# A second mixer whose recurrence is projected before its heads, and first feed-forward products taken by token tile

## The chip, the cores and the metric

The kernel runs on one core of a Trainium2 chip. TensorE (PE in the profile, its weight loads PEld), VectorE (DVE), ScalarE (ACT), GpSimd (POOL) and SyncE (SP) each work through a list of instructions of their own and wait for each other by semaphores. The metric is the time on the device of one execution, in microseconds (us). Three runs of the kernel before took 1424.63, 1426.79 and 1426.91 us; the median is 1426.79 us.

## The reference

Two transformer blocks follow each other on 256 tokens of width 1024, all in float32. The first (latent attention and stick-breaking heads, 32 experts of which each token takes four, a gated embedding) is not touched by the change but for its last norm. The second is, cut to what matters (dimension checks, transposes and casts left out):

```
def second_block(x, ...):
    h = rms_norm(x, g_pre_mix)
    q, k, v, xr, gr = split(h @ w_in)                    # five times 512 columns
    attn = moba_attention(q, k, v, rel_bias)             # 8 heads of 64; at 256 tokens plain causal
                                                         # softmax attention with a bias by distance
    xr = causal_dwconv(xr, w_conv_lru, b_conv_lru)       # 4 taps
    lru = rg_lru(xr, ...) * gelu(gr)
    mix = concatenate([attn, lru]) @ w_out               # 1024 x 1024
    x = x + rms_norm(mix, g_post_mix)
    h = rms_norm(x, g_pre_ffn)
    up = causal_dwconv(h @ w_up, w_conv_ffn, b_conv_ffn) # 5632 columns, 3 taps
    c_u, c_g = split(up)
    ffn = (gelu(c_g) * c_u) @ w_down
    return x + rms_norm(ffn, g_post_ffn)

def rg_lru(x, w_r, b_r, w_i, b_i, lam):                  # along the tokens
    r = sigmoid(x @ w_r + b_r); i = sigmoid(x @ w_i + b_i)   # block-diagonal, 8 blocks of 64
    log_a = -8 * r * softplus(-lam)
    u = sqrt(-expm1(2 * log_a)) * (i * x)
    h[t] = exp(log_a[t]) * h[t - 1] + u[t]
```

## The kernel before, in words

The tokens are two tiles of 128. Where a product has its output by feature, both token tiles stand side by side as 256 columns. A float32 operand is split into a high part in fp32r (ACT copies it, `wh` or `uh`) and the rest (`wl` or `ul`, one subtraction on DVE, L257 for weights); a product is then three matmuls, high by high, and twice high by low (`mm3`, L272 to L275). `mm_T` (L268) does so over the eight chunks of 128 inputs: 24 matmuls for 128 features. Weights come in pieces of 2 MB through a ring of three buffers, in the order of `plan` (`want`, L197 to L205); SP issues the next load when `done` frees a buffer.

The program is written in one order per step, and a scheduler that lays out the lists of all engines together moves instructions past each other where their operands allow it; `issue_after` holds some back. What stands where is seen from the lists below.

The second block runs thus. `x2_norm` (L1300) ends the first block's last norm and leaves the scale `rB` that the projections' outputs are multiplied by. `v` is projected first, then sixteen steps of `mm_T` (loop at L1465, `seq`) project `q`, `k`, `xr` and `gr`, four steps each. Two steps make a pair of 128-feature chunks, and behind a pair comes what it is for: a scaled copy to `qT` or `kT`; for `xr` the convolution (`conv`, L1347); for `gr` the gate products and the first half of the recurrence (`lru_gates`, `lru_a`). The heads are a generator (`attention`, L1439): scores `a_s`, transposes of the probabilities `a_t`, and for each pair of heads the output `a_o` into `mxh` and `mxl`; it is advanced twice behind each step of `xr` and `gr`. `lru_b` (L1374) ends the recurrence: square root, gelu, scan, gate.

`nat2` (L1202) then multiplies by `w_out`: the half with the heads (48 matmuls of 512 columns, written first), then the recurrence's half, token tile 0 before token tile 1 (24 each), and behind each tile its norm (`epi2`, L1540). While tile 1 is multiplied, DVE and ACT take tile 0 through the norms (`norm_head`, `norm_tail`, `scale3`); `turn3` (L1531) transposes it by PE and splits it to `uh`, `ul`. Between the transposes of tile 0 and those of tile 1 stand 24 matmuls into a tile that nobody reads (L1548 to L1550). The feed-forward loop follows: 44 steps `mm_T` of 256 columns, convolution, gelu, and the products with `w_down`. Its first four steps are written before the loop into `pre`. Of the first up weights, piece 0 is split by POOL, and piece 1's rest too (L1507).

Of the kernel before, what the change touches and what calls it, by code (L numbers as in the profile page):

```python
# [36 lines left out]
P = 128  # L37
# [67 lines left out]
def block_kernel(ctx: ExitStack, tc: tile.TileContext, A, out, dbg=None, parts=("t1", "moe", "over", "t3")):  # L105
# [93 lines left out]
    wo2 = A["w_o2"].rearrange("(c k p) n -> c p k n", p=P, k=4)  # L199
    for c in range(2):  # L200
        want(("o2", c), wo2[c], [P, 4, 1024])
# [994 lines left out]
    def acc_tile():  # L1196
        return psq.tile([P, 512], FT, name="acc")
# [162 lines left out]
    def lru_a(hf):  # L1360

        ms = slice(2 * hf, 2 * hf + 2)
        if hf == 0:
            held["a"] = mx_.tile([P, 4, S], FT, name="xr")
        a_ = held["a"]
        for m in (2 * hf, 2 * hf + 1):
            act(a_[:, m], rg[:, m], AF.Exp, scale=ch[:, m:m + 1], bias=ch[:, m:m + 1])
            ts(rg[:, m], rg[:, m], ch[:, m:m + 1], ch[:, m:m + 1], OP.mult, OP.add)
        stt(ig[:, ms], ig[:, ms], 1.0, xc[:, ms], OP.add, OP.mult)
        act(rg[:, ms], rg[:, ms], AF.Tanh, scale=-1.0)  # L1370
        act(xc[:, ms], a_[:, ms], AF.Square)
        stt(xc[:, ms], xc[:, ms], 1.0, rg[:, ms], OP.add, OP.mult)
# [48 lines left out]
    def a_o(p):  # L1421
        o = acc_tile()
        for kb in range(2):
# [34 lines left out]
    def presplit(j):  # L1458
        if j < len(seq):
            i, hf, m = seq[j][0]  # L1460
            sp[j] = split(ws, seq[j][1]())
            if hf == 1 and m == 1:
                done(("in2", i))

    heads = attention()  # L1465
    presplit(0)
    presplit(1)
    for j, ((i, hf, m), _) in enumerate(seq):
# [6 lines left out]
        if m == 1:  # L1475
            if i == 1:
                stt(qT[:, sl], ps, 0.125, rB2, OP.mult, OP.mult)
            elif i == 2:
                tt(kT[:, sl], ps, rB2, OP.mult)
            elif i == 3:  # L1480
                tt(xr[:, sl, 3:3 + S], ps, rB2, OP.mult)
                conv(2 * hf)
                conv(2 * hf + 1)
            else:
                tt(gr[:, sl], ps, rB2, OP.mult)
                lru_gates(2 * hf)
                lru_gates(2 * hf + 1)
                lru_a(hf)
        if i >= 3:
            next(heads, None)  # L1490
            next(heads, None)
    for _ in heads:
        pass
    lru_b()
    for m in range(4):
        act(mxh[:, 4 + m], gr[:, m])
        tt(mxl[:, 4 + m], gr[:, m], mxh[:, 4 + m].bitcast(FT), OP.subtract)
    uh, ul = new_u(t3)
# [3 lines left out]

    first = [row_split(("o2", 0), i) for i in range(4)]
    done(("o2", 0))
    wdn, wup, acts = {}, {}, {}

    def split_up(i):  # L1507
        if i >= 44:
            return
        j, m = divmod(i, 2)  # L1510
        if i in (1, 2):
            hi, lo = [mx_.tile([P, 8, P], FR, name=n) for n in (("xc", "ig"), ("rg", "vN"))[i - 1]]
            src = src_T(("up", 0), j % 2, m)
            act(hi, src)
            (G if i < 2 else V).tensor_tensor(out=lo, in0=src, in1=hi.bitcast(FT), op=OP.subtract)
            wup[i] = hi, lo
        else:
            wup[i] = split(ws, src_T(("up", j // 2), j % 2, m), eng=G if i < 1 else V)
        if i % 4 == 3:
# [20 lines left out]
    def epi2(t, acc):  # L1540
# [14 lines left out]
    for i in range(3):  # L1555
# [74 lines left out]
def host_arrays(inputs):  # L1630
# [110 lines left out]
```

## Time and profile before

| | |
|---|---|
| median of 3 runs | 1426.79 us |
| the profiled execution | 1425.2 us |
| its span | 1423.4 us |
| PE busy in the span | 1315.6 us (92%) |
| DVE busy | 627.9 us (44%) |
| ACT busy | 370.3 us (26%) |
| POOL busy | 38.9 us (3%) |
| DMA moved | 482.39 MB |

Shares of the whole span mix two parts. Up to about 1080 us the experts' weights stream in and PE waits for them; behind that the weights come faster than they are used. The change lies in the last 320 us, so the rows below are from there: windows, waits and single instructions. A matmul's duration in a row reaches to the end of its results; where matmuls follow each other, the distance from start to start is what each takes of PE.

### The profile page before, as it was taken

What the parts mean: (1) busy time and instruction counts of PE and PEld (TensorE: products, weight loads), DVE (VectorE), ACT (ScalarE), POOL (GpSimd) and SP (SyncE); (2) the same over time, 40 slices, a digit from 0 to 9 for tenths busy, and PEclk for the clock granted to TensorE, in tenths of its full rate; (3) what the DMA queues carried; (4) which work ended last, traced back from release to release, by engine and by line L of the source; (5) the groups of instructions that cost most, each with busy time, mean ns of one, the idle gap of its engine ahead of it and who ended that gap; (6) DMA issues with size and microseconds to landing.
All of it is one profiled execution on the core that took longest, in us unless ns stands there. A gap on an engine that the chain in (4) does not pass through costs nothing.

```text
span 1423.4 us, 19768 instructions
## 1 busy us (share of the span) xinstructions
PE 1315.6 (92%) x8361; PEld 741.2 (52%) x8362; DVE 627.9 (44%) x1250; ACT 370.3 (26%) x639; POOL 38.9 (3%) x53
## 2 busy tenths in 40 slices
PE   6999999999998899889999888998888998999997
PEld 6877543433433333333343333333335886899997
DVE  5576533332322223223232222322225878677776
ACT  5545310101100101001010001000014658555554
POOL 1010200000000000000000000000000101000000
PEclk9999999999999999999999999999999999999999
DMA  7339899999999999999999999999998533355530
GB/s 283 112 106 375 324 420 427 427 427 426 425 428 427 428 426 425 427 413 426 427 428 427 427 427 427 427 426 426 428 426 350 192 126 134 135 195 198 198 148 30
DMA packets 40654, 482.39 MB, mean 339 GB/s; under 512 B 4104, under 2 KB 4640, under 8 KB 12656
## 3 DMA queue, kind: packets, MB, share of 16 engines
q1 hardware_dynamic: 38944, 477.58, 80.8%
q0 software_dynamic: 752, 2.36, 0.5%
q8 instruction: 67, 1.10, 0.3%
q10 hardware_dynamic: 864, 1.13, 0.2%
q14 instruction: 27, 0.22, 0.0%
HBM read 479.99 MB, written 1.06 MB: 338 GB/s over the span
## 4 chain that ended last, share of the span: by engine, by line
DMA 47%; PE 46%; DVE 4%; ACT 1%; issue 1%; POOL 1%; DVEq 0%; SPq 0%; ACTq 0%; POOLq 0%
DMA w<-w_gu 27%; DMA w<-w_dn 19%; PE gu L978 9%; PE y L1014 5%; PE acc L273 3%; PE acc L274 3%; PE acc L275 3%; PE wk L274 3%; PE wk L275 3%; PE wk L273 3%; PE pj L273 2%; PE pj L275 2%; PE pj L274 2%; PE xg L948 1%; PE tr L993 1%
## 5 line engine op out<-in xcount | busy, mean ns | idle before, releaser
L978 PE MATMUL gu<-w,xg 128*64 128x512 f32 x2048 | 471.6, 603 | 44.7 <-DMA w<-w_gu 38.1
L978 PEld LDWEIGHTS gu<-w,xg 128*64 128x64 f32 x2048 | 142.0, 137 | 315.9 <-issue 248.9
L1014 PE MATMUL y<-w,gl 128*64 128x512 f32 x1024 | 233.1, 597 | 28.4 <-DMA w<-w_dn 26.7
L121 ACT ACTIVATE h<-gu,gs 128x512 f32<-128x512 f32 x64 | 40.5, 683 | 559.5 <-PE gu L978 559.5
L124 DVE TENSOR_TENSOR h<-sc,h 128x512 f32<-128x512 f32 x126 | 81.3, 686 | 203.2 <-PE sc L1038 200.7
L257 DVE TENSOR_TENSOR wl<-w,wh 128x1024 fp32r<-128x1024 f32 (+2 forms) x124 | 148.2, 1205 | 46.4 <-ACT wh L121 45.9
L1014 PEld LDWEIGHTS y<-w,gl 128*64 128x64 f32 x1024 | 72.9, 136 | 161.1 <-issue 156.4
L121 ACT ACTIVATE wh<-w 128x1024 fp32r<-128x1024 f32 (+2 forms) x125 | 128.3, 1038 | 96.9 <-PE acc L275 21.6
L124 DVE TENSOR_TENSOR gl<-tr,bgu 128x512 f32<-128x512 f32 x32 | 22.1, 691 | 269.5 <-PE tr L993 269.5
L274 PE MATMUL wk<-ul,wh 128*128 128x256 f32 x336 | 94.5, 281 | 0.2 <-DVE ul L124 0.2
L273 PE MATMUL wk<-uh,wh 128*128 128x256 f32 x336 | 94.5, 281 | 0.0
L275 PE MATMUL wk<-uh,wl 128*128 128x256 f32 x336 | 94.3, 281 | 0.0
L121 ACT ACTIVATE sg<-gl 128x512 f32<-128x512 f32 x32 | 20.1, 630 | 182.8 <-DVE gl L131 176.1
L274 PEld LDWEIGHTS wk<-ul,wh 128*128 128x128 f32 x336 | 63.4, 189 | 1.2 <-DVE ul L124 0.4
L273 PEld LDWEIGHTS wk<-uh,wh 128*128 128x128 f32 x336 | 63.3, 188 | 1.0 <-ACT uh L121 0.2
L275 PEld LDWEIGHTS wk<-uh,wl 128*128 128x128 f32 x336 | 63.4, 189 | 0.0
L963 DVE CAST gt<-y 128x256 fp32r<-128x256 f32 x32 | 13.6, 424 | 112.8 <-PE y L961 112.8
L948 PE MATMUL xg<-oh,u 128*128 128x64 bf16 x1536 | 50.0, 193 | 0.7 <-ACT proj L121 0.7
L948 PEld LDWEIGHTS <-u 128*128 128x128 bf16 x1536 | 49.1, 98 | 2.6 <-issue 2.3
L127 DVE SCALAR_TENSOR_TENSOR cv<-wk,vec,cv 128x255 f32<-128x255 f32 x88 | 42.2, 480 | 8.7 <-ACT cv L121 7.1
L127 DVE SCALAR_TENSOR_TENSOR sg<-y,gs,li 128x512 fp32r<-128x512 f32 x31 | 23.3, 750 | 49.9 <-ACT li L121 49.9
L121 ACT ACTIVATE li<-y,gs 128x512 fp32r<-128x512 f32 x31 | 21.3, 687 | 80.7 <-PE y L1014 79.2
(410 smaller groups left out, 1748.3 us busy)
## 6 DMA issues: line engine op xcount, KB each, us to landing
w<-w_gu SPq DMA_DIRECT2D x128, 2048.0 KB, 39.1
w<-w_dn SPq DMA_DIRECT2D x63, 2048.0 KB, 39.1
w<-w_up SPq DMA_DIRECT2D x11, 2048.0 KB, 8.1
w<-w_in SPq DMA_DIRECT2D x7, 2048.0 KB, 10.5
w<-w_down SPq DMA_DIRECT2D x5, 2048.0 KB, 7.5
w<-w_o SPq DMA_DIRECT2D x4, 2048.0 KB, 8.6
w<-w_pg SPq DMA_DIRECT2D x2, 2048.0 KB, 35.3
w<-w_in SPq DMA_DIRECT2D x2, 1024.0 KB, 9.2
```

The costliest lines, as they stand in the source:

```text
L121: return SC.activation(out=o, in_=i, func=f, **kw)
L124: return V.tensor_tensor(out=o, in0=a, in1=b, op=op)
L127: return V.scalar_tensor_tensor(out=o, in0=a, scalar=s, in1=b, op0=op0, op1=op1)
L257: eng.tensor_tensor(out=lo, in0=src, in1=hi.bitcast(FT), op=OP.subtract)
L273: PE.matmul(o, l[0], r[0], start=first, stop=False)
L274: PE.matmul(o, l[0], r[1], start=False, stop=False)
L275: PE.matmul(o, l[1], r[0], start=False, stop=last)
L948: PE.matmul(px[:, kd], u3[i][:, t, kd * P:(kd + 1) * P], oh[:, t], start=(n == 0), stop=(n == 5))
L963: V.tensor_copy(gt, pgt[:, 0:S])
L978: PE.matmul(ps[64 * s:64 * s + 64, n], xg[:, k], w[:, kk, s * 1024 + n * 512:s * 1024 + (n + 1) * 512], start=(k == 0), stop=(k == 7))
L993: PE.transpose(pt[:, m], hf[:, m * P:(m + 1) * P], ident)
L1014: i = PE.matmul(ps[64 * s:64 * s + 64], aT[:, k], w[:, kk, s * 512:(s + 1) * 512], start=(k == 0), stop=(k == 7))
```

## The change

The order of projections becomes `v`, `xr`, `gr`, then the first halves of `q` and `k`, then the second halves; the packing of `w_in2` on the host follows it. `lru_b` and its split stand behind the last step of the first halves. The heads are advanced twice behind each of the last four projection steps, and once behind each half-chunk of `w_out`'s recurrence half, which now comes first and is accumulated in four PSUM tiles held from there on. The heads' half comes second, tile 0 before tile 1 as before. The 24 matmuls of L1550 are gone; in their place `pre_up(0)` does the four first feed-forward steps for token tile 0 (128 columns), and `pre_up(1)` does them for tile 1 behind `turn3(1)`. POOL splits nothing any more: the four first up pieces are split by ACT and DVE, in buffers of the mixer. `a_o` takes its PSUM tile from the `wk` buffers, not the `acc` ones. Two small edits: `x2_norm` folds two scalings into one pass, and the recurrence's `Tanh` takes its scale and bias from columns instead of a DVE pass.

```
-    for c in range(2):
+    for c in (1, 0):
         want(("o2", c), wo2[c], [P, 4, 1024])
...
+    ts(nch, ch, -1.0, None, OP.mult)
...
     def x2_norm(t):
-        tt(xn[:, t], xn[:, t], gfin, OP.mult)
+        stt(xn[:, t], xn[:, t], r1[:, t:t + 1], gfin, OP.mult, OP.mult)
-        ts(ss, ss, r1[:, t:t + 1], r1[:, t:t + 1], OP.mult, OP.mult)
-        ts(xn[:, t], xn[:, t], r1[:, t:t + 1], None, OP.mult)
...
-            ts(rg[:, m], rg[:, m], ch[:, m:m + 1], ch[:, m:m + 1], OP.mult, OP.add)
+            act(rg[:, m], rg[:, m], AF.Tanh, scale=nch[:, m:m + 1], bias=nch[:, m:m + 1])
-        act(rg[:, ms], rg[:, ms], AF.Tanh, scale=-1.0)
...
     def a_o(p):
-        o = acc_tile()
+        o = work_tile()
...
         for h in range(8):
+            if h == 3:
+                yield
...
+    def o2_mm(i, hl, t, n, last):
+        sl = slice(n * 512, (n + 1) * 512)
+        mm3(acc2[t][n], (mxh[:, i, t * P:(t + 1) * P], mxl[:, i, t * P:(t + 1) * P]),
+            (hl[0][:, sl], hl[1][:, sl]), i == 4, last)
...
-        if i >= 3:
-            next(heads, None)
-            next(heads, None)
+        if i == 3 and m == 1 and hf == 0:
+            lru_b()
+            for k in range(4):
+                act(mxh[:, 4 + k], gr[:, k])
+                tt(mxl[:, 4 + k], gr[:, k], mxh[:, 4 + k].bitcast(FT), OP.subtract)
+        if i == 4:
+            take(2)
+
+    acc2 = [[acc_tile() for _ in range(2)] for _ in range(2)]
+    first = [row_split(("o2", 1), i) for i in range(2)]
+    for i in range(4):
+        if i + 2 < 4:
+            first.append(row_split(("o2", 1), i + 2))
+        for t in range(2):
+            for n in range(2):
+                o2_mm(4 + i, first[i], t, n, False)
+            take(1)
+    done(("o2", 1))
     for _ in heads:
         pass
-    lru_b()
-    for m in range(4):
-        act(mxh[:, 4 + m], gr[:, m])
-        tt(mxl[:, 4 + m], gr[:, m], mxh[:, 4 + m].bitcast(FT), OP.subtract)
...
-            idle = work_tile()
-            for _ in range(24):
-                PE.matmul(idle, mxh[:, 0, 0:P], mxh.rearrange("p k n -> p (k n)")[:, 0:512], start=True, stop=True)
+            pre_up(0)
             norm_tail(t, y, r, x2, x2)
             scale3(t)
             turn3(t)
 
+    def pre_up(t):
+        tl = slice(t * P, (t + 1) * P)
+        for i in range(4):
+            mm_T(pre[i // 2][i % 2][:, tl], wup[i], uh[:, :, tl], ul[:, :, tl])
...
-    nat2([("o2", 0), ("o2", 1)], tok(mxh, mxl), epi2, first)
+    sp = [row_split(("o2", 0), i) for i in range(4)]
+    done(("o2", 0))
+    split_up(2)
+    split_up(3)
+    for t in range(2):
+        for n in range(2):
+            for i in range(4):
+                o2_mm(i, sp[i], t, n, i == 3)
...
+        epi2(t, acc2[t])
...
-    for i in range(4):
-        mm_T(pre[i // 2][i % 2], wup[i], uh, ul)
+    pre_up(1)
```

What the engines' lists make of it is shown at three places. First PE around the last two heads. `as` are probabilities (transposed at L1416 before, L1415 now), `pT` their transposes, `vN` the values, `acc<-wh,uh` with 512 columns are products of `w_out`. Before:

```order
L1356 MATMUL acc<-xc,wri 128x256 x4
L1416 MATMUL wk<-cf,as 128x128 x6
L1429 MATMUL acc<-pT_9144,vN 64x256
L273 MATMUL acc<-wh,uh 128x512
L274 MATMUL acc<-wl,uh 128x512
L275 MATMUL acc<-wh,ul 128x512
L273 MATMUL acc<-wh,uh 128x512
L274 MATMUL acc<-wl,uh 128x512
L1429 MATMUL acc<-pT_9150,vN 64x256
L1432 MATMUL acc<-pT_9144,vN 64x128
L1432 MATMUL acc<-pT_9150,vN 64x128
```

Now:

```order
L274 MATMUL acc<-wl,uh 128x512
L275 MATMUL acc<-wh,ul 128x512
L1415 MATMUL wk<-cf,as 128x128
L1428 MATMUL wk<-pT_9227,vN 64x256
L1415 MATMUL wk<-cf,as 128x128 x2
L273 MATMUL acc<-wh,uh 128x512
L274 MATMUL acc<-wl,uh 128x512
L275 MATMUL acc<-wh,ul 128x512
L1428 MATMUL wk<-pT_9235,vN 64x256
L1431 MATMUL wk<-pT_9227,vN 64x128
L1431 MATMUL wk<-pT_9235,vN 64x128
```

Before, both last heads' transposes stood together ahead of nearly all of `w_out`; now the last head's stand inside it, with products in front and between.

Second, PE between `w_out` and the feed-forward loop; `cf` is the identity that transposes, `qT` and `xr` name the buffers in which tiles 0 and 1 of the normed input lie, `wk<-uh,wh` are products of the up weights. Before:

```order
L275 MATMUL acc<-wh,ul 128x512
L1535 MATMUL wk<-cf,qT 128x128 x8
L1550 MATMUL wk<-uh 128x512 x24
L1535 MATMUL wk<-cf,xr 128x128 x8
L273 MATMUL wk<-uh,wh 128x256
L273 MATMUL wk<-uh,rg 128x256
L274 MATMUL wk<-ul,wh 128x256
L275 MATMUL wk<-uh,wl 128x256
L273 MATMUL wk<-uh,wh 128x256
```

Now, from the end of `w_out` on, and then at the end of the products of tile 0:

```order
L275 MATMUL acc<-wh,ul 128x512
L1554 MATMUL wk<-cf,qT 128x128 x8
L273 MATMUL wk<-uh,wh 128x128
L273 MATMUL wk<-uh,rg 128x128
L274 MATMUL wk<-ul,wh 128x128
L275 MATMUL wk<-uh,wl 128x128
L273 MATMUL wk<-uh,wh 128x128
```

```order
L274 MATMUL wk<-ul,gr 128x128
L275 MATMUL wk<-uh,wri 128x128
L1554 MATMUL wk<-cf,xr 128x128 x8
L273 MATMUL wk<-uh,wh 128x128
L273 MATMUL wk<-uh,rg 128x128
L274 MATMUL wk<-ul,wh 128x128
L275 MATMUL wk<-uh,wl 128x128
```

Between the two groups of transposes stand 96 products of 128 columns where 24 empty ones of 512 were, and another 96 follow the second group, where there were 96 of 256.

Third, ACT while the first block's last tile is turned; `uh<-wk` are turned pieces that PE's `v` products use, `junk` are the square sums of the norms, `wh<-w` weight splits. Before:

```order
L121 ACTIVATE tmp<-acc,rp 128x512
L121 ACTIVATE junk_8372,ss<-h 128x1024
L121 ACTIVATE wh<-w 128x1024 x2
L121 ACTIVATE uh<-wk,gc_8042 128x128
L121 ACTIVATE tmp<-acc,rp 128x512
L121 ACTIVATE wh<-w 128x1024
L121 ACTIVATE uh<-wk,gc_8042 128x128
L121 ACTIVATE junk,ss_8385<-h 128x512
L121 ACTIVATE wh<-w 128x1024
L121 ACTIVATE junk,ss_8385<-h 128x512
```

Now:

```order
L121 ACTIVATE tmp<-acc,rp 128x512
L121 ACTIVATE wh<-w 128x1024 x3
L121 ACTIVATE uh<-wk,gc_8044 128x128
L121 ACTIVATE tmp<-acc,rp 128x512
L121 ACTIVATE junk_8374,ss<-h 128x1024
L121 ACTIVATE uh<-wk,gc_8044 128x128
L121 ACTIVATE junk,ss_8385<-h 128x512 x2
L121 ACTIVATE uh<-wk,gc_8044 128x128
L121 ACTIVATE wh<-w 128x1024
L121 ACTIVATE uh<-wk,gc_8044 128x128
```

Three weight splits now stand together ahead of the first turned piece of this stretch, and a square sum of 1024 columns stands between the pieces.

## Rows read from the trace of the kernel before

**Rows 1.** Stages of the second block: us, engines busy (count), PE clock, DMA share, GB/s.

```profile
core 0: us, PE busy (x) PEld busy (x) DVE busy (x) ACT busy (x) POOL busy (x), PEclk, DMA share, GB/s
...
1131.00:1152.40 21.40, 21.40 (x182) 21.28 (x182) 14.58 (x15) 7.57 (x8) 0.00 (x0) 1.00 0.70 251
1157.00:1188.40 31.40, 31.25 (x214) 25.29 (x214) 27.48 (x76) 21.36 (x50) 0.00 (x0) 1.00 0.24 85
1188.40:1209.00 20.60, 16.54 (x73) 11.88 (x72) 16.64 (x23) 15.29 (x26) 5.36 (x2) 0.99 0.28 102
...
1256.00:1383.00 127.00, 127.00 (x904) 119.54 (x903) 93.47 (x136) 71.24 (x106) 0.00 (x0) 1.00 0.49 190
```

**Rows 2.** Timeline of PE, heads to norm: start, us, instruction [idle before].

```profile
1191.71 0.70 PE L1416 MATMUL wk<-cf,as 128*128 128x128 f32 x3 [1.28 <-DVE as L131]
...
1207.54 0.50 PE L274 MATMUL acc<-wl,uh 128*128 128x512 f32 x1 [2.05 <-DVE wl L257]
...
1209.05 1.22 PE L273 MATMUL acc<-wh,uh 128*128 128x512 f32 x2 [0.78 <-ACT wh L121]
```

**Rows 3.** Window behind the waits, with the granted PE clock.

```profile
1209.00:1212.00 3.00, 2.95 (x7) 2.37 (x8) 3.00 (x4) 1.90 (x2) 0.00 (x0) 0.50 0.00 0
```

**Rows 4.** Timeline of DVE and of POOL, end of the recurrence.

```profile
1196.61 0.69 DVE L124 TENSOR_TENSOR gr<-rg,gr 128x512 f32<-128x512 f32 x1 [2.05 <-ACT gr L121]
...
1199.44 0.42 DVE L124 TENSOR_TENSOR ul<-gr,uh 128x256 fp32r<-128x256 f32 x1
...
1200.96 2.58 DVE L124 TENSOR_TENSOR ul<-gr,uh 128x256 fp32r<-128x256 f32 x1
...
1203.46 2.89 DVE L124 TENSOR_TENSOR gr<-rg,gr 128x512 f32<-128x512 f32 x1
...
1206.27 1.21 DVE L257 TENSOR_TENSOR wl<-w,wh 128x1024 fp32r<-128x1024 f32 x1
...
1200.44 2.81 POOL L257 TENSOR_TENSOR wl<-w,wh 128x1024 fp32r<-128x1024 f32 x1 [70.62 <-ACT wh L121]
1203.22 2.58 POOL L1515 TENSOR_TENSOR ig<-w,xc 128x1024 fp32r<-128x1024 f32 x1
```

**Rows 5.** Timeline of PE between `w_out` and the feed-forward loop.

```profile
1221.26 1.32 PE L1535 MATMUL wk<-cf,qT 128*128 128x128 f32 x8 [0.23 <-DVE qT L127]
1222.33 5.70 PE L1550 MATMUL wk<-uh 128*128 128x512 f32 x24
1228.20 1.38 PE L1535 MATMUL wk<-cf,xr 128*128 128x128 f32 x8 [0.17 <-DVE xr L127]
1229.54 0.39 PE L273 MATMUL wk<-uh,wh 128*128 128x256 f32 x1
...
1230.27 0.39 PE L274 MATMUL wk<-ul,wh 128*128 128x256 f32 x1 [0.22 <-DVE ul L124]
```

**Rows 6.** Timeline of ACT and of PE around `x2_norm`.

```profile
1110.88 1.06 ACT L121 ACTIVATE junk<-h 128x1024 f32<-128x1024 f32 x1
...
1126.67 0.39 PE L275 MATMUL acc<-uh,wl 128*128 128x256 f32 x1 [0.41 <-DVE wl L257]
```

**Rows 7.** Weight loads and float32 products: timeline, line 833, timeline, page.

```profile
151.55 1.87 PEld L833 LDWEIGHTS c<-wr,h 128*128 128x128 f32 x16
...
L833 PEld LDWEIGHTS c<-wr,h x16: 190/192/192, 151.6 to 153.2; 128*128 128x128 f32 x16
...
1176.50 1.89 PE L1356 MATMUL acc<-xc,wri 128*128 128x256 f32 x8
...
L274 PEld LDWEIGHTS wk<-ul,wh 128*128 128x128 f32 x336 | 63.4, 189 | 1.2 <-DVE ul L124 0.4
...
L948 PEld LDWEIGHTS <-u 128*128 128x128 bf16 x1536 | 49.1, 98 | 2.6 <-issue 2.3
```

**Rows 8.** Timeline of DVE, tile 0's `ul` and tile 1's `xr`.

```profile
1223.12 1.28 DVE L124 TENSOR_TENSOR ul<-wk,uh 128x512 fp32r<-128x512 f32 x2
...
1227.39 1.41 DVE L127 SCALAR_TENSOR_TENSOR xr<-h,rf,kT 128x512 f32<-128x512 f32 x2 [0.66 <-POOL rf L295]
```

More of the change, by code (lines that the diff above doesn't have):

```diff
@@ L685, in block_kernel @@
     ts(ch, ch, -4.0, None, OP.mult)
+    nch = keep.tile([P, 4], FT, name="nch")
+    ts(nch, ch, -1.0, None, OP.mult)
     relb = sm.tile([E, 8], FT, name="relb", bufs=1)
@@ L1463, in presplit, with take @@
                 done(("in2", i))
+    def o2_mm(i, hl, t, n, last):
+        sl = slice(n * 512, (n + 1) * 512)
+        mm3(acc2[t][n], (mxh[:, i, t * P:(t + 1) * P], mxl[:, i, t * P:(t + 1) * P]),
+            (hl[0][:, sl], hl[1][:, sl]), i == 4, last)
+    def take(n):
+        for _ in range(n):
+            next(heads, None)
     heads = attention()
@@ L1476, in block_kernel @@
             if i == 1:
[L1477 to L1480, printed above, removed]
                 tt(xr[:, sl, 3:3 + S], ps, rB2, OP.mult)
@@ L1483, in block_kernel @@
                 conv(2 * hf + 1)
-            else:
+            elif i == 2:
                 tt(gr[:, sl], ps, rB2, OP.mult)
@@ L1488, in block_kernel @@
                 lru_a(hf)
-        if i >= 3:
-            next(heads, None)
-            next(heads, None)
+            elif hf == 0:
+                stt(qT[:, 2 * i - 6:2 * i - 4], ps, 0.125, rB2, OP.mult, OP.mult)
+            else:
+                tt(kT[:, 2 * i - 6:2 * i - 4], ps, rB2, OP.mult)
+        if i == 3 and m == 1 and hf == 0:
[15 more added lines that the diff above has]
+    done(("o2", 1))
     for _ in heads:
         pass
-    lru_b()
-    for m in range(4):
-        act(mxh[:, 4 + m], gr[:, m])
-        tt(mxl[:, 4 + m], gr[:, m], mxh[:, 4 + m].bitcast(FT), OP.subtract)
     uh, ul = new_u(t3)
@@ L1501, in block_kernel @@
     SY.dma_start(gpre, row_ap(A["g_pre_ffn"], D))
-    first = [row_split(("o2", 0), i) for i in range(4)]
-    done(("o2", 0))
     wdn, wup, acts = {}, {}, {}
@@ L1510, in split_up @@
         j, m = divmod(i, 2)
-        if i in (1, 2):
-            hi, lo = [mx_.tile([P, 8, P], FR, name=n) for n in (("xc", "ig"), ("rg", "vN"))[i - 1]]
+        if i in (1, 2, 3):
+            hi, lo = [mx_.tile([P, 8, P], FR, name=n) for n in (("xc", "ig"), ("rg", "vN"), ("gr", "wri"))[i - 1]]
             src = src_T(("up", 0), j % 2, m)
             act(hi, src)
-            (G if i < 2 else V).tensor_tensor(out=lo, in0=src, in1=hi.bitcast(FT), op=OP.subtract)
+            tt(lo, src, hi.bitcast(FT), OP.subtract)
             wup[i] = hi, lo
         else:
-            wup[i] = split(ws, src_T(("up", j // 2), j % 2, m), eng=G if i < 1 else V)
+            wup[i] = split(ws, src_T(("up", j // 2), j % 2, m))
         if i % 4 == 3:
@@ L1553, in epi2 @@
             turn3(t)
-    for i in range(3):
-        split_up(i)
-    nat2([("o2", 0), ("o2", 1)], tok(mxh, mxl), epi2, first)
+    def pre_up(t):
+        tl = slice(t * P, (t + 1) * P)
+        for i in range(4):
+            mm_T(pre[i // 2][i % 2][:, tl], wup[i], uh[:, :, tl], ul[:, :, tl])
+    for i in range(2):
+        split_up(i)
+    pre = []
+    sp = [row_split(("o2", 0), i) for i in range(4)]
[6 more added lines that the diff above has]
+                o2_mm(i, sp[i], t, n, i == 3)
+        if t == 1:
+            for j in range(2):
+                pre.append([p_[:, m] for p_ in [work_tile().rearrange("p (a b) -> p a b", a=2)] for m in range(2)])
+        epi2(t, acc2[t])
     dump("x3", x2)
     acc = [[acc_tile() for _ in range(2)] for _ in range(2)]
-    pre = []
-    for j in range(2):
-        pre.append([p_[:, m] for p_ in [work_tile().rearrange("p (a b) -> p a b", a=2)] for m in range(2)])
     def split_down(j):
@@ L1592, in ffn_down @@
                     (hi[:, n * 512:(n + 1) * 512], lo[:, n * 512:(n + 1) * 512]), j == 0, j == 21)
-    with tc.issue_after(held["hi"].ins), tc.issue_after(held["turn"].ins):
-        split_up(3)
-    for i in range(4):
-        mm_T(pre[i // 2][i % 2], wup[i], uh, ul)
+    pre_up(1)
     cmix.close()
@@ L1685, in host_arrays @@
     q, k, v, xr, gr = (w[:, i * 512:(i + 1) * 512] for i in range(5))
-    f["w_in2"] = c(np.concatenate([rows(v), pairs(q), pairs(k), pairs(xr), pairs(gr)], axis=0))
+    qk2 = [np.stack([colchunks(q, 256)[i], colchunks(k, 256)[i]], axis=1)[None] for i in range(2)]
+    f["w_in2"] = c(np.concatenate([rows(v), pairs(xr), pairs(gr)] + qk2, axis=0))
     f["rel_bias"] = c(g["rel_bias_2"])
```

## The prediction

> **What bounds the kernel now.** I read the table of stages first. After the expert stage, from about 1095 us to the end, TensorE (PE) bounds the kernel: in the projections it is busy 21.40 of 21.40 us, in the feed-forward loop 127.00 of 127.00 [rows 1]. So a change in the second block is worth the time for which PE waits, runs at the lower clock, or does work that nothing needs, and costs what it adds to PE. In the heads beside `xr` and `gr` PE is busy 31.25 of 31.40 us, though VectorE (DVE) has 27.48 us of work there; right behind them, PE loses 4 of 20.60 us [rows 1].
>
> The waits of PE name the places [rows 2]: 1.28 us for a head's probabilities `as`, 2.05 us for a weight split `wl` on DVE, 0.78 us for `wh` on ScalarE (ACT). After the last two the granted clock is 0.50 for the 3 us from 1209 to 1212 [rows 3], 1.2 of 2.4 GHz; without that the same products take 1.50 us less. I count the fall to the two waits in front of it, 2.05 and 0.78 us with two products between them; the wait of 1.28 us was followed by none.
>
> Why `wl` was late: it stood on DVE behind two steps of the recurrence's end. `ul<-gr` took 2.58 us, the same form just before 0.42; `gr<-rg,gr` took 2.89 against 0.69; GpSimd (POOL) ran two subtractions of its own from 1200.44 to 1205.80 [rows 4].
>
> Then the turn from norm to feed-forward [rows 5]: transposes of tile 0 at 1221.26, 24 empty products of 5.70 us, transposes of tile 1 at 1228.20 with a wait of 0.17 us for `xr` from DVE, steady products from 1230.27.
>
> **The change, part by part.** (1) Recurrence first, heads beside half of `w_out`. The recurrence needs `xr` and `gr`, so with these two projected first its tail stands beside the last six of the sixteen projection steps instead of behind them all; its half of `w_out` comes first, and the last heads get that half's 48 wide products beside them. Removed: 1.28 + 2.05 + 0.78 + 1.50 = 5.61 us. The cover is PE work of the same amount as before: neither projections nor `w_out` products nor heads change in number. DVE's work is moved, not grown: the two POOL subtractions become two `wl` of 1.21 us [rows 4], and PE stood still for none of the heads but the last where DVE was 88% busy. What is late next is the last pair of heads: the last head's transposes stand 12 wide products behind those of the head before it, and 3 more come before the pair's output, 15 x 0.23 = 3.4 us in all (0.23 from the empty ones, 5.70 / 24 [rows 5]). I take no wait there; its price is rival 3. SP loads `o2` halves in the other order, same bytes, and issues `g_pre_ffn` later; `up` loads queue behind it, but the first was in long before. Taken at nothing, cover: those loads are wanted after 1230.
>
> (2) `x2_norm` loses one pass over 128x1024 and a small product on DVE, beside PE's `v` products; one wait there was 0.41 us [rows 6], so at best 0.4 is won. Against it, ACT's order changes: `uh` of tile 1 now stands behind a square sum of 1.06 us [rows 6] that PE's next product would see in full. Between -0.4 and +1.2 I take 0, since which is last is not in the trace. The fused Tanh and `nch` move 0.41 us pieces from DVE to ACT under projections: nothing; uncovered they would cost 4 x 0.4.
>
> (3) `pre_up`. The 96 first feed-forward products of 256 columns become two times 96 of 128 columns; 24 empty ones go. The going saves nothing by itself: the transposes of tile 1 waited for DVE's `xr`, not for PE. What counts is the price of a narrow fp32r product, which no row shows. Wide ones go 182 in 21.40 us, 0.1176 each [rows 1]. Each needs its own 128x128 weight load, and PE's loads are busy 21.28 of 21.40. Where the columns are few, 16 records of the router's product with 32 columns follow each other in (1.87 - 0.19) / 15 = 0.112 us, with a load of 192 ns each [rows 7]. The fp32r load lasts 189, the bf16 load 98 [rows 7]; so fp32r loads like float32, and I take the loads' pitch, 0.112: halving the columns saves next to nothing. Bounds: half of the wide pitch, 0.0588, below; the plain float32 product above, 4 of 256 columns in 1.89 us [rows 7], half of 0.47 or 0.236.
>
> The Trainium skill, "TensorE: Matmul & The Clock Gate", says in its section on weight-path perf modes that the fast weight load needs 128 weights and a type that is not FP32; the 189 against 98 ns fit fp32r being counted as FP32 there. With the fast load the lower bound would hold.
>
> The sum: the first half of `ul` for tile 0 is done at 1223.12 + 0.64, say 1223.8 [rows 8]; 96 x 0.112 = 10.75 brings PE to 1234.55. The tile-1 transposes stand behind these in PE's order, so they start then and not at 1228.20. From transposes to steady products took 2.07 us [rows 5]: 1236.62; two products are done by then, 94 x 0.112 = 10.53 end at 1247.15. Before: 1230.27 + 94 x 0.1176 = 1241.32. So this part costs 5.83 us. The rest of the loop starts when both tiles are through, so nothing gives it back: ACT and DVE get slack there that PE does not use.
>
> Sum: -5.61 + 5.83 = +0.2 us. The profiled execution took 1425.2 us (span 1423.4), so 1425.4; that execution lay 1.6 us under the median, and in the median's terms the forecast is 1426.8 + 0.2 = **1427.0**. Its own range: pitch 0.105 or a front gain gives 1 to 2 less, other short seams about 1 more of gain, 1423.5; a pitch no better than the wide one (+1.1), a clock at 0.50 for 3 us, as in [rows 3], after the 1.5 us that PE has next to nothing to do before the first narrow product (+1.5) and the front (+1.2) give 1431.
>
> **Rivals.** 1, faster: weight loads overlap each other and the narrow product goes at half the wide pitch. Then 96 x 0.0588 = 5.64 end at 1229.4, transposes 1.2 late, end 1231.5 + 5.5 = 1237.0, 4.3 earlier than before: -9.9, 1416.9. Against it: loads at 99% busy and the 0.112 at 32 columns. For it: those rows are float32, two records per product, not fp32r. The same skill page, section on the back-to-back issue gap, gives about 81 ns per matmul at 128 columns in streams with loads; by that, an estimate, pre_up would come out even with before and the time at 1421.1.
>
> 2, slower: a narrow fp32r product costs like float32, 0.236: 22.7 us to 1246.5, 2.07, 22.2 to 1270.7, +29.4, so 1450.6. Nothing in the trace has this type below 256 columns, so it can't be shut out; the loads' lengths are no sign of it.
>
> 3, slower: the heads beside `w_out` wait as the last one did. Four of them stand there, 4 x 1.28 = 5.1: 1432.1. It decides from the point where DVE's heads and splits together want more than PE's products there. For it: DVE gets some ten splits of 1.21 us beside them, and scores, transposes and outputs now share the four PSUM buffers of one name. Against: 88% DVE load cost PE 0.15 us before.
>
> That the waits simply don't go is the same as 3 in time.
>
> **Chances.** Forecast 0.52, rival 1 0.24, rival 2 0.08, rival 3 0.16. About 0.2%, 2.9 us, is what a measurement of this kernel can tell from no change. Of the forecast 0.08 lies faster, 0.36 within, 0.08 slower; rival 1 is faster, 2 slower, 3 mostly slower (0.13). Faster 0.32, same 0.39, slower 0.29. The range 1417 to 1433 leaves out rival 2 and the far end of rival 1.
>
> **What would show it.** The pitch of `wk<-uh,wh 128x128` products: near 0.11 the forecast, near 0.06 rival 1, over 0.2 rival 2. The tile-1 transposes wait for no DVE tile. The rows with 2.05, 0.78 and 1.28 us are gone, no clock under 1 between heads and norm, and POOL has no long subtraction. Waits of PE for `as` or `pT2` between `w_out` products would be rival 3. A clock of 0.5 behind tile 0's transposes would add what the range holds for it.

## The result, and the profile after

The changed kernel takes 1446.17 us, the median of 20 runs (1426.38 to 1451.6), against 1427.57 us for the kernel before in the same sessions (20 runs, 18 of them from 1423.77 to 1431.42 us and two far out, 1523.57 and 4292.38). The ratio is 1.0087 (95% interval 1.0062 to 1.0112); it leaves out runs over 1.5% above the fastest of their kernel, here five from 1448.35 us up. The ratio of the medians is 1.013; as the times stand in two groups, either figure alone says little. The forecast was 1427.0 us with a range of 1417 to 1433. The two groups are these: six runs lie between 1426.38 and 1431.78 us at a mean granted TensorE clock of 0.989 to 0.993, and thirteen between 1445.40 and 1451.6 us at 0.974 to 0.981; one is between them, 1435.67 at 0.988. The profiled execution is one of the thirteen, 1445.4 us.

The head of its page, and the granted clock in 40 slices:

```profile
span 1443.8 us, 19903 instructions
...
PEclk9999999999999999999999999999999999599999
```

The digit 5, in the slice from 1227 to 1263 us (the 35th of 36.1 us each), is where the 20 us are. Windows of that stretch, in the columns of [rows 1], the first of them for comparison with the heads and `w_out` of before:

```profile
1190.00:1210.00 20.00, 20.00 (x96) 13.34 (x96) 13.48 (x32) 9.10 (x23) 0.00 (x0) 1.00 0.41 144
1217.00:1220.00 3.00, 1.98 (x13) 1.43 (x13) 3.00 (x7) 1.66 (x4) 0.55 (x1) 1.00 0.22 93
1220.00:1223.00 3.00, 3.00 (x25) 3.00 (x24) 1.73 (x4) 1.39 (x4) 0.34 (x1) 0.82 0.00 0
1223.00:1259.00 36.00, 35.96 (x169) 35.54 (x168) 8.65 (x9) 6.04 (x7) 0.21 (x1) 0.50 0.16 59
1259.00:1262.00 3.00, 3.00 (x15) 3.00 (x15) 0.73 (x2) 1.02 (x2) 0.58 (x1) 0.50 0.02 5
1262.00:1265.00 3.00, 3.00 (x24) 3.00 (x23) 2.70 (x7) 1.43 (x3) 0.00 (x0) 0.85 0.46 175
```

Where PE was busy 16.54 of 20.60 us before [rows 1], it is now busy 20.00 of 20.00: the hole is gone there, as forecast (how much of that is the order's doing, experiments 10 and 12 show). From 1223 to 1259 PE is busy 35.96 of 36 us, at a granted clock of 0.50, 1.2 of 2.4 GHz. With the parts of the windows around, (1 - clock) times their lengths is 0.54 + 18 + 1.5 + 0.45 = 20.5 us; 1445.4 less this is 1424.9, and the profiled execution of before took 1425.2. PE's timeline where the clock fell:

```profile
1217.18 1.38 PE L1554 MATMUL wk<-cf,qT 128*128 128x128 f32 x8 [0.50 <-DVE qT L127]
...
1219.71 0.33 PE L274 MATMUL wk<-ul,wh 128*128 128x128 f32 x1 [0.74 <-DVE ul L124]
...
1221.77 0.27 PE L274 MATMUL wk<-ul,wh 128*128 128x128 f32 x1
...
1222.04 0.42 PE L273 MATMUL wk<-uh,wh 128*128 128x128 f32 x1
```

The transposes of tile 0 wait 0.50 us for DVE's `qT`, the first low product 0.74 us for `ul`. Then the narrow products run 0.11 us apart, until at 1222 each takes 0.41 us instead of 0.27 and they stand 0.21 apart. And where it rose again:

```profile
1260.21 0.41 PE L275 MATMUL wk<-uh,wri 128*128 128x128 f32 x1
1260.43 0.52 PE L273 MATMUL wk<-uh,wh 128*128 128x256 f32 x1
...
1263.01 0.28 PE L273 MATMUL wk<-uh,wh 128*128 128x256 f32 x1
```

The last narrow product starts at 1260.21 and the first of 256 columns at 1260.43; 2.6 us behind it the products are short again (0.28 us). All 192 narrow products were over before the clock came back.

The other signs that the prediction named: POOL has no subtraction left beside the recurrence, and the two forms that took 2.58 and 2.89 us in [rows 4] are short (DVE's timeline):

```profile
1162.47 0.69 DVE L124 TENSOR_TENSOR gr<-rg,gr 128x512 f32<-128x512 f32 x1 [1.68 <-ACT gr L121]
...
1166.54 0.40 DVE L124 TENSOR_TENSOR ul<-gr,uh 128x256 fp32r<-128x256 f32 x1
```

All waits of PE from 1095 to 1275 us (in total, times, longest):

```profile
PE acc L273 <- ACT uh L121: 1.0, 1, 1.0
PE acc L275 <- DVE wl L257: 0.9, 1, 0.9
PE wk L274 <- DVE ul L124: 0.7, 1, 0.7
PE wk L1554 <- DVE qT L127: 0.5, 1, 0.5
```

Those of [rows 2] are gone; none is for `as` or for a transposed head. New are 0.95 us for a turned piece `uh` on ACT (the page of waits rounds it to 1.0), and 0.90 for a split in the middle of the projections. The first stands behind the square sum that the prediction's step (2) named, 1.06 us of ACT just ahead of the piece:

```profile
1114.22 1.06 ACT L121 ACTIVATE junk<-h 128x1024 f32<-128x1024 f32 x1
...
1115.27 0.36 ACT L121 ACTIVATE uh<-wk,gc 128x128 fp32r<-128x128 f32 x1
```

### The profile page after: what moved, and what is told of

The parts are those of the page before. It is cut to its first block, busy times and chain, and to the rows that moved or that the text cites. A ratio compares the mean times of both kernels' runs of the same rounds, so it can differ in the third digit from the quotient of the medians.

```text
span 1443.8 us, 19903 instructions
## 1 busy us (share of the span) xinstructions
PE 1341.4 (93%) x8433; PEld 765.0 (53%) x8434; DVE 622.7 (43%) x1245; ACT 373.3 (26%) x642; POOL 31.2 (2%) x51
## 3 DMA queue, kind: packets, MB, share of 16 engines
q10 hardware_dynamic: 864, 1.13, 0.3%
HBM read 479.99 MB, written 1.06 MB: 333 GB/s over the span
## 4 chain that ended last, share of the span: by engine, by line
PE 49%; DMA 44%; DVE 4%; ACT 2%; issue 1%; POOL 0%; DVEq 0%; SPq 0%; ACTq 0%; POOLq 0%
DMA w<-w_gu 22%; DMA w<-w_dn 21%; PE gu L980 10%; PE y L1016 6%; PE wk L274 4%; PE wk L275 4%; PE wk L273 4%; PE acc L273 3%; PE acc L274 3%; PE acc L275 3%; PE pj L273 2%; PE pj L275 2%; PE pj L274 2%; PE xg L950 1%; PE tr L995 1%
## 5 line engine op out<-in xcount | busy, mean ns | idle before, releaser
L274 PE MATMUL wk<-ul,wh 128*128 128x256 f32 (+1 forms) x336 | 95.8, 285 | 0.8 <-DVE ul L124 0.7
L273 PE MATMUL wk<-uh,wh 128*128 128x256 f32 (+1 forms) x336 | 96.0, 286 | 0.0
L275 PE MATMUL wk<-uh,wl 128*128 128x256 f32 (+1 forms) x336 | 95.8, 285 | 0.0
L127 DVE SCALAR_TENSOR_TENSOR cv<-wk,vec,cv 128x255 f32<-128x255 f32 (+1 forms) x88 | 41.8, 480 | 19.2 <-ACT cv L121 17.7
```

The costliest lines, as they stand in the source:

```text
L127: return V.scalar_tensor_tensor(out=o, in0=a, scalar=s, in1=b, op0=op0, op1=op1)
L273: PE.matmul(o, l[0], r[0], start=first, stop=False)
L274: PE.matmul(o, l[0], r[1], start=False, stop=False)
L275: PE.matmul(o, l[1], r[0], start=False, stop=last)
```

## The experiments

Three theories for the 20 us. **N**: a stream of narrow products lets the clock fall by itself. **W**: the short waits at the turn, which the empty products used to fill, let it fall, and a narrow stream merely keeps the clock that it finds. **X**: the new order of the mixer does it. Every kernel below is timed against the kernel before on the same chip.

**1. The new order with wide products and empty ones.**

```
-            pre_up(0)
+            idle = work_tile()
+            for _ in range(24): PE.matmul(idle, ...)       # 512 columns, as before
...
-    pre_up(1)
+    for i in range(4):
+        mm_T(pre[i // 2][i % 2], wup[i], uh, ul)
```

> The changed kernel with its first feed-forward products as they were: 96 of 256 columns behind the second tile's transposes, and the 24 empty products in the gap; the other parts of the change stay. Theory N (the stream of narrow products itself lets TensorE's clock fall and keeps it at 0.50 until wide products come): no fall, clock 1.00 from the heads to the loop; the time is that of before less what the front shows in the changed profile (the turn begins 3.3 us earlier by the traces), so before minus 2 to 4 us, 1423 to 1425. Theory W (the waits of 0.50 and 0.74 us at the turn let it fall, and narrow products only fill the time): the same here, since the empty products stand in those waits. Theory X (the new order of projections, heads and w_out causes the fall, whatever follows): clock 0.50 again behind the turn and 1440 us or more.

Measured: 1422.57 us, ratio 0.9979 (0.9970 to 0.9988), 3.0 us less than before; the granted clock is 1.00 from 1190 to 1256 us. X falls: the loss comes with part (3) of the change, the narrow products and the empty ones taken out.

**2. The same without the empty products.** Only the loop of 24 is left out of the kernel above.

> As the one with wide products, but with nothing in the gap between the two tiles' transposes, so that TensorE stands still there for some 6 us. Theory N: the clock falls in or behind that gap, and comes back 2 to 3 us after the wide products begin, as it did in the changed kernel (2.2 us): at half speed for that stretch, 1 to 2 us are lost, 1424 to 1427. Theory W: the same fall, and as the wait is five times as long, at least the same loss. What it tells apart is how much of the 20 us can come from an idle engine alone: over 5 us more than the kernel with the empty products would speak against N.

Measured: 1423.2 us, 0.9983 (0.9974 to 0.9993): only 0.6 us more than with the empty ones, the intervals overlapping, and a little under the 1424 to 1427 that N gave. PE's timeline behind the gap:

```profile
1224.49 1.94 PE L1554 MATMUL wk<-cf,xr 128*128 128x128 f32 x8 [5.58 <-DVE xr L127]
1226.26 0.58 PE L273 MATMUL wk<-uh,wh 128*128 128x256 f32 x1
...
1229.48 0.28 PE L273 MATMUL wk<-uh,wh 128*128 128x256 f32 x1
```

PE stood still for 5.58 us, the clock fell (products of 0.41 to 0.58 us), and 3.2 us after the first of 256 columns at 1226.26 they are back at 0.28. The fall ahead of wide products was soon over. A wait of 5.58 us, over four times the two of the changed kernel together, cost 0.6 us here, so waiting alone doesn't make the 20 us.

**3. Narrow products, with the waits filled.**

```
             y, r = norm_head(t, acc, gpm)
+            for _ in range(4): PE.matmul(acc2[0][0], ...)   # 512 columns, read by nobody
             with tc.issue_after(held["head"].ins):
                 turn3(0)
+            for _ in range(6): PE.matmul(acc2[0][1], ...)
             pre_up(0)
```

> The changed kernel with 10 empty products of 512 columns more: 4 ahead of the first tile's transposes and 6 behind them, so that TensorE goes from wide products into the narrow ones with no wait between. Theory W: the clock stays at 1.00, and the time is the changed kernel's without the fall, 1427 + 10 x 0.23 - 1.24 of waits, about 1428. Theory N: the clock falls within the first stream of 96 narrow products all the same and stays at 0.50 until wide products come: 1440 to 1450.

Measured: 1427.51 us, 1.0015 (1.0006 to 1.0024), all 11 runs between 1425.64 and 1429.65. PE's timeline at the turn, and a window of the 192 narrow products that follow (they start from 1221.68 to 1244.82, the rest of the window is the loop):

```profile
1218.40 1.09 PE L1566 MATMUL acc<-uh 128*128 128x512 f32 x4
1219.33 1.11 PE L1554 MATMUL wk<-cf,qT 128*128 128x128 f32 x8
1220.20 1.65 PE L1570 MATMUL acc<-uh 128*128 128x512 f32 x6
1221.68 0.22 PE L273 MATMUL wk<-uh,wh 128*128 128x128 f32 x1
```

```profile
1222.00:1252.00 30.00, 29.47 (x259) 29.09 (x257) 15.80 (x25) 13.08 (x22) 1.12 (x2) 1.00 0.25 88
```

No wait at tile 0's turn, and no fall: the same narrow products, begun at full clock, keep it for all their 23 us. Two waits of 0.25 and 0.28 us do stand among them, behind tile 1's transposes (1233.66 and 1234.38), and the clock holds there too; experiments 6, 7 and 8 have the same two and hold at that place as well. This is W's case and against N.

**4. Narrow products elsewhere, in the kernel before.** Projection steps 0 to 3 in two halves.

```
-        mm_T(ps[:, m], w, u2h, u2l)
+        for hs in ([slice(0, P), slice(P, S)] if j < 4 else [slice(0, S)]):
+            mm_T(ps[:, m, hs], w, u2h[:, :, hs], u2l[:, :, hs])
```

> The kernel before, with only the first four of the sixteen projection steps done in two halves of 128 columns: 192 narrow products for 96 wide ones, in a stretch in which TensorE waits for nothing ahead, and which neither the new order nor the turn touches. At full clock 192 x 0.111 - 96 x 0.1176 = +10.0 us. Theory W: no wait, no fall, +10, 1437. Theory N: the clock falls in the stream and stays at 0.50 to its end, as 192 narrow products at half clock take 0.213 each: between +10 and +30, near +25, 1445 to 1457.

Measured: 1456.63 us, 1.0220 (1.0206 to 1.0234), +31 us, at the far end of what N gave. The edit was not what I took it for: the first narrow products need only tile 0, so PE runs ahead, and then waits for tile 1's scale. PE's timeline and windows:

```profile
1127.45 0.33 PE L275 MATMUL acc<-uh,wl 128*128 128x128 f32 x1 [0.47 <-DVE wl L257]
...
1131.65 0.49 PE L327 MATMUL wk<-cf,rb 128*128 128x128 f32 x2 [2.08 <-DVE rb L131]
```

```profile
1132.00:1135.00 3.00, 3.00 (x18) 3.00 (x17) 2.06 (x3) 0.00 (x0) 0.00 (x0) 0.53 0.82 236
1135.00:1168.00 33.00, 33.00 (x157) 33.00 (x156) 4.37 (x4) 3.17 (x3) 0.00 (x0) 0.50 0.30 119
```

Waits of 0.47 and 2.08 us stand among the narrow products; the clock is down at once behind the second, and stays at 0.50 through the rest of them, to 1173 us. Of the 31 us that is 20.5 (half of 41), and the narrow products' own price is the other 10. By itself this fits N and W alike.

**5. The same with steps 4 to 7**, which have 96 wide products ahead of them and no wait (`if 4 <= j < 8`).

> The kernel before with the fifth to eighth projection steps in two halves of 128 columns (192 narrow products for 96 wide ones), a stretch with 96 wide products ahead of it and no wait at its start: what the earlier one with the first four steps did not have, since there a wait of 2.08 us stood among the narrow products. Theory W (a wait lets the clock fall, a narrow stream keeps the clock that it finds, wide products bring it back): no fall, 192 x 0.111 - 96 x 0.1176 = +10.0 us against before, about 1436. Theory N (the narrow stream alone lets it fall): clock 0.50 in the stretch, +18 to +30, over 1443.

Measured: 1436.73 us, 1.0072 (1.0049 to 1.0094), +10.3 us where W gave +10.0. A window around the narrow products, which start from 1136.11 to 1157.38:

```profile
1130.00:1160.00 30.00, 30.00 (x267) 30.00 (x266) 13.44 (x14) 7.42 (x7) 0.00 (x0) 1.00 0.55 197
```

Busy without a gap, clock 1.00. N falls: the stream alone doesn't bring the clock down.

**6. Only the wait behind the transposes filled**: 4 empty products after `turn3(0)` in the changed kernel (the scheduler moved one of them in among the transposes).

> The changed kernel with 4 empty products of 512 columns among and behind the first tile's transposes, so that the wait of 0.74 us for the split is filled, and the wait of 0.50 us ahead of the transposes is left. Theory W with either wait enough: the clock still falls, in some executions or all, 1435 to 1448. Theory W with both needed, or the later one alone to blame: no fall, 1427 to 1428. Theory N: falls, 1446.

Measured: 1427.09 us, 1.0003 (0.9992 to 1.0015), 12 runs from 1425.87 to 1431.05. PE's timeline and the window:

```profile
1218.51 0.94 PE L1568 MATMUL acc<-uh 128*128 128x512 f32 x3
...
1219.90 0.33 PE L274 MATMUL wk<-ul,wh 128*128 128x128 f32 x1 [0.28 <-DVE ul L124]
```

```profile
1216.00:1256.00 40.00, 38.68 (x313) 36.86 (x312) 24.57 (x40) 19.58 (x34) 2.21 (x4) 1.00 0.22 84
```

Four empty products of 0.23 us each take 19 us off the changed kernel by the medians; the wait of 0.50 us ahead of the transposes is still there, the one for `ul` is down from 0.74 to 0.28 us. The four products fill most of that wait, and they are also wide work right ahead of the narrow one; which of the two keeps the clock, the runs don't tell apart.

**7. Only the wait ahead of the transposes filled**: 4 empty products before `turn3(0)`.

> The changed kernel with 4 empty products of 512 columns ahead of the first tile's transposes, so that the wait of 0.50 us is filled, and the wait of 0.74 us between transposes and products is left. Theory W with either wait enough: the clock still falls, in some executions or all, 1435 to 1448. Theory W with both needed, or the earlier one alone to blame: no fall, 1427 to 1428. Theory N: falls, 1446.

Measured: 1445.91 us, 1.0083 (1.0043 to 1.0123), in two groups as the changed kernel: four of 12 runs from 1425.19 to 1427.64 us, eight from 1445.14 to 1448.17. So it is the place behind the transposes that counts: the same four products ahead of them didn't keep the clock in most runs. Its profile is of one of the four that held:

```profile
1217.55 0.33 PE L273 MATMUL wk<-uh,wh 128*128 128x128 f32 x1 [0.17 <-ACT uh L121]
...
1218.53 0.33 PE L274 MATMUL wk<-ul,wh 128*128 128x128 f32 x1 [0.54 <-DVE ul L124]
```

```profile
1216.00:1256.00 40.00, 38.75 (x319) 37.23 (x318) 25.03 (x40) 19.03 (x33) 1.67 (x3) 1.00 0.18 70
```

With 0.17 and 0.54 us of waits in this place the clock held. What decides in which executions it falls, the runs don't show.

**8. A wide stretch between the two narrow ones**: 24 empty products held back until tile 0's narrow products are issued.

> The changed kernel with 24 empty products of 512 columns between the first tile's 96 narrow products and the second tile's transposes; the waits at the turn stay. Theory W: where the clock falls at the turn, it stays at 0.50 through the first 96 narrow products, comes back 2 to 3 us into the empty ones, and the second 96 narrow products go at 1.00: some 10 us lost to the fall and 6 to 7 to the empty products, 1441 to 1445 (1433 in executions without the fall). Theory N: the second narrow stream lets it fall again, 1448 to 1455.

Measured: 1442.81 us, 1.0118 (1.0093 to 1.0142). Its windows, the empty products from 1238 to 1245.7:

```profile
1223.00:1238.00 15.00, 15.00 (x72) 15.00 (x72) 1.41 (x2) 0.00 (x0) 0.41 (x1) 0.50 0.01 1
1238.00:1241.00 3.00, 3.00 (x8) 2.42 (x9) 0.00 (x0) 0.00 (x0) 0.00 (x0) 0.50 0.00 0
1241.00:1244.00 3.00, 3.00 (x11) 2.35 (x11) 0.00 (x0) 0.00 (x0) 0.00 (x0) 0.73 0.00 0
1244.00:1258.00 14.00, 13.46 (x111) 12.72 (x110) 7.06 (x7) 5.81 (x7) 0.00 (x0) 1.00 0.19 64
```

As W has it: 0.50 through the first stream, back some 4.6 us into the empty products, where W gave 2 to 3 (0.73 from 1241 to 1244 is 1.6 us at 0.50), and 1.00 through the second narrow stream.

**9. The kernel before with part (3) alone**: `pre_up` for both tiles, the empty products out, a fourth up piece split ahead of `w_out`.

> The kernel before with only the third part of the change: 2 x 96 products of 128 columns for the 96 of 256, the first tile's in place of the empty products, with the fourth up piece split earlier on DVE; order of projections, heads and w_out, the GpSimd splits and x2_norm as before. Theory W: without the empty products TensorE waits some 0.7 us for the first tile's split, as in the changed kernel, and the clock falls there in most executions: 1443 to 1450, and about 1431 (+5) in those where it does not. If the fall needs the new order too: 1430 to 1432 in all.

Measured: 1445.84 us, 1.0135 (1.0102 to 1.0168), six runs, none near the 1431 us of a kernel without the fall. The median is the middle of a hole: three runs lie from 1438.77 to 1441.28 (mean clock 0.982 to 0.987) and three from 1450.39 to 1453.62 (0.973 to 0.978), and none within W's 1443 to 1450. An estimate: 96 narrow products at 0.213 us instead of 0.112 cost 9.7 us, so 1431 and a fall through one of the two streams is 1440.7, through both 1450.4. The profile is of an execution of the upper group; no trace shows one of the lower. Windows at the turn, where PE waits 1.13 us for `qT` and 0.74 for `ul`, and behind it:

```profile
1223.00:1227.00 4.00, 3.26 (x22) 3.15 (x22) 2.87 (x6) 1.66 (x5) 0.20 (x1) 0.80 0.00 0
1227.00:1263.00 36.00, 35.97 (x169) 35.54 (x169) 8.65 (x9) 6.03 (x7) 0.34 (x1) 0.50 0.16 59
```

The clock falls with the old order too; X is out from this side as well.

**10. The best of the new order**: experiment 1 with `x2_norm` as before.

> The kernel with the new order, wide products and empty ones (1422.57 us), with x2_norm as in the kernel before. Theory S (the waits of 0.95 us for a turned piece on ACT and 0.90 us for a split, where before had one of 0.41 us, come from x2_norm's new order on ACT): both go, 1.4 us less, about 1421. Rival (they come from the new order of projections, whose splits now stand elsewhere): nothing, 1422 to 1423.

Measured: 1420.67 us, 0.9965 (0.9952 to 0.9978), 1.9 less than experiment 1 by the medians, on another chip (the intervals of the ratios overlap). Its largest wait of PE:

```profile
PE acc L275 <- DVE wl L257: 1.3, 2, 0.9
```

The wait of 0.95 for ACT is gone, the one of 0.90 for a split is not (it is the larger of the two in 1.3). So theory S holds for the first only; the second is there with the old norm too, and so goes with the other parts of the change.

**11. The kernel before with the new `x2_norm` alone.**

> The kernel before with x2_norm as in the changed one, and nothing else. Theory S: the wait of 0.95 us for a turned piece on ACT appears, and with it up to 1.4 us more than before. Rival (the norm edit is free, as the prediction took it): the same as before within 0.5 us, and no such wait.

Measured: 1426.82 us, 1.0007 (0.9997 to 1.0016), 1.0 us more by the ratio, not clear of nothing. But the wait is there, as in the changed kernel, and the one of 0.41 us for `wl` [rows 6] is gone:

```profile
PE acc L273 <- ACT uh L121: 1.0, 1, 1.0
```

**12. The kernel before without GpSimd's subtractions.**

```
-            (G if i < 2 else V).tensor_tensor(out=lo, in0=src, in1=hi.bitcast(FT), op=OP.subtract)
+            tt(lo, src, hi.bitcast(FT), OP.subtract)
...
-            wup[i] = split(ws, src_T(("up", j // 2), j % 2, m), eng=G if i < 1 else V)
+            wup[i] = split(ws, src_T(("up", j // 2), j % 2, m), eng=V)
```

> The kernel before with the two subtractions of GpSimd done by DVE and nothing else. Theory P (GpSimd's subtractions, beside which DVE's took 2.58 and 2.89 us where the same forms took 0.42 and 0.69, made the split late for which TensorE waited 2.05 us and then 0.78): both short again, DVE gains 4.4 us and gets 2.4 us more to do, so the wait of 2.05 falls to under 1 and the clock stays up behind it: 2 to 4 us less than before. Rival (the wait comes from the recurrence's tail standing behind the last projections): waits and clock as before, and no gain.

Measured: 1420.64 us, 0.9971 (0.9961 to 0.9980), 4.1 us less by the ratio. DVE's timeline at the recurrence's end, PE's remaining waits there, and the window:

```profile
1202.58 0.40 DVE L124 TENSOR_TENSOR ul<-gr,uh 128x256 fp32r<-128x256 f32 x1
1202.90 0.68 DVE L124 TENSOR_TENSOR gr<-rg,gr 128x512 f32<-128x512 f32 x1
```

```profile
1193.33 0.70 PE L1416 MATMUL wk<-cf,as 128*128 128x128 f32 x3 [1.28 <-DVE as L131]
...
1208.84 0.51 PE L274 MATMUL acc<-wl,uh 128*128 128x512 f32 x1 [1.08 <-DVE wl L257]
```

```profile
1190.00:1210.00 20.00, 17.64 (x79) 13.13 (x79) 16.02 (x27) 17.14 (x28) 0.00 (x0) 1.00 0.29 105
```

The two forms take 0.40 and 0.68 us instead of 2.58 and 2.89, the wait for `wl` is 1.08 instead of 2.05 (theory P gave under 1), that for `wh` is gone, and the clock stays at 1.00, though the wait of 1.28 for `as` is as before.

Experiments 10 and 12 and the kernel before have two waits of PE in the same places, one in the first projection step and one behind the second tile's transposes. PE's timelines of experiment 12, then of experiment 10:

```profile
1128.27 0.39 PE L275 MATMUL acc<-uh,wl 128*128 128x256 f32 x1 [0.41 <-DVE wl L257]
...
1228.60 0.38 PE L274 MATMUL wk<-ul,wh 128*128 128x256 f32 x1 [0.22 <-DVE ul L124]
```

```profile
1126.43 0.38 PE L275 MATMUL acc<-uh,wl 128*128 128x256 f32 x1 [0.41 <-DVE wl L257]
...
1225.55 0.38 PE L274 MATMUL wk<-ul,wh 128*128 128x256 f32 x1 [0.22 <-DVE ul L124]
```

From the one to the other it took 103.60 us before (1126.67 to 1230.27, [rows 6] and [rows 5]), 100.33 in experiment 12 and 99.12 in experiment 10. So of 4.5 us in this stretch 3.3 come without the new order.

## Why the prediction was wrong

**The step that failed** is the clock term of the forecast's own range: "a clock at 0.50 for 3 us, as in [rows 3], after the 1.5 us that PE has next to nothing to do before the first narrow product (+1.5)". The place was right, and the cause as far as the runs go: the fall comes there, and four products in the wait behind the transposes keep it off (experiments 3, 6 and 7). The length was not: in the profiled execution it lasted 41 us and cost 20, and by their times some 14 of the 20 executions had it. I took the 3 us from [rows 3], where what followed the waits were products of 512 columns, and experiment 2 shows that this was right for wide products: there a fall costs 0.6 us by the medians. Behind the turn stood 192 products of 128 columns, and on those the clock, once down, came back in no profile here (the lower runs of experiment 9 and the one of the changed kernel at 1435.67 us, shorter falls by their times, left no trace); it did 2.5 to 5.0 us behind the first wider ones (in the changed kernel and experiments 2, 4, 8 and 9). Why narrow products don't bring it back stays open, and so does what decides whether an execution falls. And a term of 20 us by its size belonged among the rivals with a chance of its own, at first place: its start was a wait that I had counted.

Part (3) said that the going of the empty products "saves nothing by itself". At full clock that is so, but it took out what kept the clock: where they stand, or only 4 of them behind the transposes, the clock holds.

**The price of a narrow product**, step (3), was right: 0.112 us at full clock, 16 in 1.79 us of the changed kernel (1219.98 to 1221.77), against 0.112 forecast from the router's rows. Rivals 1 and 2 (0.0588 and 0.236) fall. By the prediction's own sign, a pitch over 0.2, most of the profiled stream would speak for rival 2, and its 1450.6 us lies close to the time measured; only the granted clock tells them apart, since the 0.213 us stand at 0.50 and the 0.112 at 1.00. The reason given, that the weight loads set the pitch, fits (PEld is busy 3.00 of 3.00 us from 1220 to 1223), but no run tests it. The Trainium skill, "TensorE: Matmul & The Clock Gate", section on the back-to-back issue gap, gives about 81 ns at 128 columns; in these fp32r products the measurement decides, 112 ns. From the transposes of tile 0 to the first loop product it took 25.39 us in experiment 7's trace and 20.22 in experiment 1's, 5.2 us more; forecast 5.83.

**The reordering**, step (1), was right in size and for the most part wrong in its reason. Experiment 10 has the new order, no GpSimd subtractions and the old norm, and lies 5.0 us (3.1 to 6.8) under before; forecast 5.61. But experiment 12, on the same chip in the same session, has the old order and only leaves out the GpSimd subtractions, and lies 4.1 us (2.9 to 5.6) under before. What the new order adds to this is 0 by the medians (1420.67 and 1420.64), within some 2 us, and 1.2 us by the two traces: it removes the waits of 1.28 us for the last head and of 1.08 for `wl`, and gets one of 0.90 for a split in exchange. The prediction had read the stretched DVE rows and GpSimd's, and yet booked their going under the order. The Trainium skill, "Trainium Architecture — The Big Picture", section on what this means for kernel authors, says that DVE and GpSimd contend for a shared port, with an exclusive lock; 2.89 us beside GpSimd and 0.68 without it agree.

**The norm**, step (2), taken at 0 between -0.4 and +1.2, brought the wait of 0.95 us by the mechanism named against it, in the changed kernel and in experiment 11, and also the gain that it hoped for: the wait of 0.41 us is gone in both. Net that is some 0.5 us of PE's waits. The times say 1.0 us (experiment 11, not clear of nothing) and 1.9 us (experiments 1 and 10, on two chips); what they show beyond the waits is not explained.

**Rival 3** didn't occur: no wait for the heads beside `w_out`.

So for executions without the fall the sum comes out: the six runs of the changed kernel in the lower group take 1426.38 to 1431.78 us, and experiment 6, with the clock held, 1427.09 for a forecast of 1427.0, of which 0.5 us is what the 4 empty products (4 x 0.23) cost beyond the wait (0.46) that they fill. Part of that is luck, since the 5.61 us were booked to the wrong edit. And it is no credit to the forecast: the likeliest course was the one that it priced at 1.5 us.

Four versions beat both kernels, by 0.17 to 0.35% against the kernel before: experiments 1, 2, 10 and 12. The last needs only two small edits of the kernel before.

## What to carry to other kernels

Before taking out work that "nobody needs" on TensorE, look at what follows it: if the clock falls in the wait that it leaves, wide products brought it back here within 5 us, and a stream of narrow ones kept it down to the stream's end. Cutting 256 columns into two times 128 nearly doubled the cost here, since a product of half the columns took 0.112 us against 0.120. And book a gain to the one edit that removes its cause: taken one at a time, the small edit on GpSimd was worth 4 us and the large one on the order 1.2 by the traces, and nothing that the times could show.

## What the runs showed of the hardware

- At a granted clock of 0.50, products of 128 and of 256 columns both stood 0.213 us apart (two from 1259.79 to 1260.21, seven from 1260.75 to 1262.24 in the changed kernel); at 1.00, 0.112 and 0.120 (24 from 1263.01 to 1265.89). At the lower level halving the columns gained nothing, at the higher 7%.
- PE can be busy 35.96 of 36 us by its records at a clock of 0.50 and not get the full clock back, and 29.47 of 30 at 1.00 (experiment 3, its narrow products and the start of the loop) and not lose it.
- One and the same program fell or held from run to run: by their times 6 of 20 held in the changed kernel, 4 of 12 in experiment 7, all 12 in experiment 6, none of six in experiment 9.
- Products of 512 columns stood 0.228 us apart in the profiled execution of before (1216.06 to 1220.40) and 0.233 in that of the changed kernel (1213.02 to 1216.05), both at a clock of 1.00. This is no chance of one execution: from 1210 us to the end the mean is 0.229 us in the traces of before and of all five kernels made from it, and 0.233 to 0.235 in those of the changed kernel and of all seven made from that, though experiments of both kinds ran on the same chips. What in the program does it stays open. Over that stretch the two kinds of kernel come out alike: from the second wait shown under experiment 12 to the end of the span it is 193.1 us before and in experiment 12, and 193.4 in experiment 10.
